# A hybrid encoder trunk on one Trainium2 core: another axis order for two copies, and a fused final norm

## The chip, the cores and the metric

The kernel runs on one core of a Trainium2 chip. The metric is the device time of one execution in microseconds (us). Before the change three executions took 2153.46, 2158.15 and 2160.55 us; the median is 2158.15 us. Engines are named as in the profile: PE is TensorE's matrix multiply and PEld its weight load, DVE is VectorE, ACT is ScalarE, POOL is GpSimd, SP is SyncE.

## The reference

For 256 tokens of width 2048 (all float32) the reference computes one layer and a final norm:

```
h = x + W_out[ norm(conv(.)) || norm(S5(.)) ](rmsnorm(x))
h = h + MemCrossAttn(rmsnorm(h), rmsnorm(mem))
h = h + PEER(rmsnorm(h))
out = rmsnorm(h)            # h * rsqrt(mean(h*h) + eps) * final_norm_g
```

The change touches PEER and the final norm. PEER has a table of 16384 experts, each with an input row u and an output row v of 2048 numbers. For each token, 8 heads choose 16 experts each, so a token has 128 chosen experts:

```
u = take(u_tab, it)                       # 128 rows of 2048 a token
act = gelu(einsum("td,tkd->tk", xt, u))
v = take(v_tab, it)
out = einsum("tk,tkd->td", gt * act, v)
```

## The kernel before

**The tokens** are handled as two tiles of 128, numbered 0 and 1 (`tt` in the code). Expert number e is written as block b = e // 128 and row r = e % 128.

**Two ways to the same scores.** Of the 2048 columns of u, the last 1280 are gathered row by row: `dot` (L857 to L862) issues an indirect DMA on POOL's queue and one multiply-and-sum on DVE, 256 times, 128 for each tile. The first 768 columns are not gathered. `dense` (L882 on) instead reads all 128 blocks of the table, transposes them on PE, and multiplies them with all tokens. This gives a score for every pair of an expert and a token, and they are kept in SBUF as `W[tt]`, 128 partitions (the row r) by 128 blocks by 128 tokens, the token innermost: `WA` for tile 0, `WB` for tile 1. Each pair of blocks ends with two ACT copies from PSUM, one for each tile (L901).

**Picking the wanted scores.** `extract` (L904) takes four tokens of a tile (a group; there are 32 groups for each tile). It loads the tokens' expert numbers with a DMA on SP's queue into one of five buffers (`id_at`), makes a selection matrix `E` on ACT (L908, L909), and multiplies it on PE with the scores of one token at a time: `W[tt][:, :, token]`, 128 by 128, is the stationary operand (L912). In that slice the 128 blocks of one token lie 128 numbers (512 bytes) apart. The result `y` goes to one of three PSUM buffers. `pick` (L916) then selects on DVE (`hit`, L920) and sums on PE (L922).

**Writing the coefficients back.** When a tile's scores are picked and the gathered part is added, `finish` gives the coefficients. `build` (L925) spreads them over a matrix of all experts, again four tokens at a time: two comparisons on DVE (L929), four scalings by a coefficient, on ACT (L936) or on DVE (L938), four products on PE (L939), and one ACT copy from PSUM into `W[tt]` (L940). The product has the token outermost and the block innermost. The copy walks in that order, so it reads PSUM in sequence and writes SBUF at steps of 512 bytes. `W[tt]` thus holds scores first and coefficients later, in the same memory.

**Order.** `settle` mixes these steps: first extract and pick for tile 0; then, for tile 1, extract, pick and `build` of tile 0's coefficients in turn. These steps are interleaved with the gathered dots: after every dot `Pace` lets 2.4 steps go, starting at dot 185 of 256 (`SETTLE_AT`, `SETTLE_RATE`). DVE's order is fixed by this program order (`manual_schedule`); the order on the other engines is chosen by the scheduler when the program is built. After the last dot, tile 1's coefficients are built in a loop by themselves (L1012 on). There, scalings alternate between ACT and DVE (`R_BY[1] = 'AVAV'`); in tile 0's builds all four are ACT's.

**The output side.** A last long loop over the 128 blocks reads the v table and multiplies it with the coefficients, `W[tt][:, b, :]`, split into high and low parts (L1062, L1063), with 18 products a block (L1072 to L1074). 576 of v's columns are gathered into `accg`, the other 1472 (three column pieces of 512, 512 and 448) are summed in PSUM.

**The final norm** (L1079 on) follows for each tile: add the PSUM sums to the residual (L1082, DVE), squares with a row sum (L1083, L1084, ACT), multiply by the gain `gF` (L1085, L1087; DVE, the last piece POOL), sum, square root and reciprocal (L1088, L110, L111), multiply by the row's scale (L1092 on ACT or L1094 on DVE), and four output DMAs on SP's queue (L1095).

Of the kernel before, what the change touches and what calls it, by code (L numbers as in the profile page):

```python
# [9 lines left out]
F32 = mybir.dt.float32  # L10
# [4 lines left out]
AF = mybir.ActivationFunctionType  # L15
ALU = mybir.AluOpType
# [4 lines left out]
P = 128  # L21
T = 256
NTT = T // P
# [29 lines left out]
DC = D - GC  # L53
COLS = [slice(c, min(c + 512, DC)) for c in range(0, DC, 512)]
NCH = len(COLS)
# [16 lines left out]
def trunk(ctx, tc, a, out, dbg=None):  # L72
    nc = tc.nc
    V, S, G, PE, SY = nc.vector, nc.scalar, nc.gpsimd, nc.tensor, nc.sync

    def bc(ap, shape):
        return ap.to_broadcast(shape)

    consts = ctx.enter_context(tc.tile_pool(name="consts", bufs=1))
    small = ctx.enter_context(tc.tile_pool(name="small", bufs=4))  # L80
# [28 lines left out]
    def rstd_of(dst, ssq, n):  # L109
        S.activation(dst, ssq, AF.Sqrt, bias=eps_t[: dst.shape[0]], scale=1.0 / n)  # L110
        V.reciprocal(dst, dst)  # L111
# [9 lines left out]
    with ExitStack() as wctx:  # L121
# [74 lines left out]
        with ExitStack() as mctx:  # L196
# [165 lines left out]
            for i, nm in enumerate(("ssm_c_re", "ssm_c_im")):  # L362
# [3 lines left out]
                for w in range(2):  # L366
                    V.tensor_scalar(cbd[:, :, w, :], craw, par[:, w:w + 1], -1.0 if i else 1.0, op0=ALU.mult,
                                    op1=ALU.mult)
# [192 lines left out]
            for k in range(CW):  # L561
                for q in range(CQ):
                    src = cpad[:, q, k:k + T]
                    if k == 0:
                        V.tensor_scalar(acc[:, q, :], src, cwT[:, q, 0:1], colv[:, 0, q:q + 1], op0=ALU.mult,
                                        op1=ALU.add)
                    else:
                        V.scalar_tensor_tensor(acc[:, q, :], src, cwT[:, q, k:k + 1], acc[:, q, :],  # L568
                                               op0=ALU.mult, op1=ALU.add)
# [4 lines left out]
            for q in range(CQ):  # L574
                S.activation(acc[:, q, :], acc[:, q, :], AF.Silu, bias=colv[:, 2, q:q + 1],
                             scale=colv[:, 1, q:q + 1])
# [287 lines left out]
    NQ = P // 4  # L864
# [11 lines left out]
    W = [wa_p.tile([P, NB, P], F32, name="WA"), WB]  # L876
# [5 lines left out]
    def dense():  # L882
        for b in range(NB):
            if b == free_blocks - free_blocks % 2:
                while (1, len(GROUPS[1]) - 1) not in ready:
                    yield
            raw = lr_p.tile([P, DU], F32, name="raw", bufs=4)
            SY.dma_start(raw, a["peer_u"][b * P:(b + 1) * P, :DU])
            pt = psu.tile([P, KD, P], F32, name="ut")
            for k in range(KD):  # L890
                PE.transpose(pt[:, k, :], raw[:, k * P:(k + 1) * P], ident)  # L891
            ut = lr_p.tile([P, KD, P], F32, name="ut", bufs=2)
            S.copy(ut, pt)  # L893
            if b % 2 == 0:
                ps = psu.tile([P, 2, T], F32, name="sy")
            for k in range(KD):
                PE.matmul(ps[:, b % 2, :], ut[:, k, :], hnT[:, k, :], start=k == 0 and b % 2 == 0,  # L897
                          stop=k == KD - 1 and b % 2 == 1, skip_group_check=True)
            if b % 2:
                for tt in range(NTT):  # L900
                    S.copy(W[tt][:, b - 1:b + 1, :], ps[:, :, tt * P:(tt + 1) * P])  # L901
            yield

    def extract(route, g):  # L904
        ids = id_at[(route.tt * NQ + g) % len(id_at)]
        SY.dma_start(ids.rearrange("p i s k -> p i (s k)"), ib_dram[route.tt][g:g + 1].to_broadcast([P, 4, 2 * NSLOT]))
        E = lr_p.tile([P, 4, P], F32, name="E", tag="ut", bufs=2)
        S.activation(E, ids[:, :, 1, :], AF.Abs, bias=part[:, 1:2], scale=1.0)  # L908
        S.activation(E, E, AF.Relu, bias=1.0, scale=-1.0)  # L909
        y = psu.tile([P, 4, P], F32, name="y", tag=("sy", "sy", "pw")[g % 3], bufs=(2, 2, 1)[g % 3])  # L910
        for i in range(4):
            PE.matmul(y[:, i, :], W[route.tt][:, :, i * NQ + g], E[:, i, :], start=i == 0, stop=i == 3,  # L912
                      skip_group_check=True)
        return ids, y

# [9 lines left out]
    def build(route, g, by, tag, bufs):  # L925
        ts = slice(4 * g, 4 * g + 4)
        LR = [lr_p.tile([P, 4, P], F32, name=nm, tag="raw", bufs=4) for nm in "RL"]
        for x, at in zip(LR, (0, 1)):
            V.tensor_tensor(x, bc(iota[:, None, :P], [P, 4, P]), bc(route.tr[:, at, ts, None], [P, 4, P]),  # L929
                            op=ALU.is_equal)  # L930
        R, L = LR
        pw = psu.tile([P, 4, P], F32, name="pw", tag=tag, bufs=bufs)
        for i in range(4):
            c = route.cT[:, 4 * g + i:4 * g + i + 1]
            if by[i] == "A":
                S.activation(R[:, i, :], R[:, i, :], AF.Copy, scale=c)  # L936
            else:
                V.tensor_scalar(R[:, i, :], R[:, i, :], c, None, op0=ALU.mult)  # L938
            PE.matmul(pw[:, i, :], L[:, i, :], R[:, i, :], start=i == 0, stop=i == 3, skip_group_check=True)  # L939
        S.copy(W[route.tt][:, :, ts].rearrange("p b t -> p t b"), pw)  # L940

    routes = [Route(0), None]
    ready = set()
# [26 lines left out]
    def settle():  # L970
        groups = P // 4
        for tt in range(NTT):
            held = {}
            for n in range(groups + LAG):
                if n < groups:
                    held[n] = extract(routes[tt], n)
                    yield
                if n >= LAG:
                    pick(routes[tt], n - LAG, *held[n - LAG])
                    yield  # L980
                if tt and n < groups:
                    build(routes[0], n, R_BY[0], "ut", 2)
                    yield
            if tt == 0:
                while tick[0] <= NSLOT:
                    yield
                yield from routes[0].finish()
# [5 lines left out]
    order = ctx.enter_context(ExitStack())  # L993
    order.enter_context(tc.manual_schedule(engines={mybir.EngineType.DVE}))
    dense_gen = dense()
    paces = [Pace(routing, ROUTE_RATE), Pace(dense_gen, DENSE_RATE)]
    tick = [0]
# [18 lines left out]
    for g in range(P // 4):  # L1016
        build(routes[1], g, R_BY[1], ("sy", "ut")[g % 2], 2)
# [10 lines left out]
    accg = [vs.tile([P, GC], F32, name=f"accg{tt}", bufs=1) for tt in range(NTT)]  # L1028
# [13 lines left out]
    def used(tt, i):  # L1042
        b = 8 + i * (D // P)
        return W[tt][:, b:b + D // P, :].rearrange("p b t -> p (b t)")

    h3, sq = ([used(tt, i) for tt in range(NTT)] for i in range(2))
    gF = used(0, 2)
# [28 lines left out]
            next(gathering)  # L1076
            done += 1

    for tt in range(NTT):  # L1079
        st = small.tile([P, NCH + 3], F32, name="rms_st")  # L1080
        for c, cs_ in enumerate(COLS):
            V.tensor_add(h3[tt][:, cs_], h3[tt][:, cs_], acc[tt][:, c, :cs_.stop - cs_.start])  # L1082
            S.activation(sq[tt][:, cs_], h3[tt][:, cs_], AF.Square, accum_out=st[:, c:c + 1])  # L1083
        S.activation(sq[tt][:, DC:], accg[tt], AF.Square, accum_out=st[:, NCH:NCH + 1])  # L1084
        V.tensor_mul(h3[tt][:, DC:], accg[tt], gF[:, DC:])  # L1085
        for c, cs_ in enumerate(COLS):
            (G if c == NCH - 1 else V).tensor_mul(h3[tt][:, cs_], h3[tt][:, cs_], gF[:, cs_])  # L1087
        V.tensor_reduce(st[:, NCH + 1:NCH + 2], st[:, :NCH + 1], axis=AX.X, op=ALU.add)  # L1088
        rstd_of(st[:, NCH + 2:NCH + 3], st[:, NCH + 1:NCH + 2], D)
        for c, cs_ in enumerate([slice(DC, D)] + COLS):  # L1090
            if c % 2:
                S.activation(sq[tt][:, cs_], h3[tt][:, cs_], AF.Copy, scale=st[:, NCH + 2:NCH + 3])  # L1092
            else:
                V.tensor_scalar(sq[tt][:, cs_], h3[tt][:, cs_], st[:, NCH + 2:NCH + 3], None, op0=ALU.mult)  # L1094
            SY.dma_start(out[tt * P:(tt + 1) * P, cs_], sq[tt][:, cs_])  # L1095


# [27 lines left out]
```

## Time and profile before

| what | us |
|---|---|
| three executions | 2158.15, 2160.55, 2153.46 |
| the profiled execution, device time | 2160.26 |
| its span, first to last instruction | 2158.2 |
| PE busy | 1985.0 (92%) |
| DVE busy | 1778.4 (82%) |
| ACT busy | 1028.6 (48%) |
| POOL busy | 751.2 (35%) |

The change touches these stretches of the span. The dense products run from about 885 to 1327 us. Tile 0's groups are extracted and picked from 1327 to 1427 us. Tile 1's groups, together with tile 0's builds, take until about 1566 us. Tile 1's builds take until 1621 us. The output loop follows until 2142 us, and the final norm ends the span. Busy shares are averages over all of it, so a stage's own rows count.

### The profile page before, as it was taken

How to read it: one execution, taken by the hardware profiler on the slowest of the kernel's cores; microseconds unless marked ns; L12 is line 12 of the kernel's file. 1: busy time of each engine (PE TensorE's matmuls, PEld its weight loads, DVE VectorE, ACT ScalarE, POOL GpSimd, SP SyncE). 2: the span in 40 equal slices, each digit the busy share in tenths (PEclk: the TensorE clock that was granted, in tenths of full speed). 3: DMA queues.
4: the chain of work that ended last, by engine and by line, in shares of the span. 5: the costliest groups of instructions: out<-in, count | busy, mean ns of one | idle time of the engine just before them, and what ended most of it. 6: DMA issues, size and time to landing. Idle time of an engine off the chain costs nothing.

```text
span 2158.2 us, 31798 instructions
## 1 busy us (share of the span) xinstructions
PE 1985.0 (92%) x11459; PEld 1714.8 (79%) x11459; DVE 1778.4 (82%) x2905; ACT 1028.6 (48%) x1683; POOL 751.2 (35%) x548
## 2 busy tenths in 40 slices
PE   8998898999999999799999997888868999999997
PEld 7987786677799888788878886777656888888886
DVE  5789999977666557999976667788897999899997
ACT  5764454446445445233333322468794444444444
POOL 0000000000000003444456666332207877677773
PEclk9999899999999999899999998798999999999998
DMA  7654444554965568799999999987618999999995
GB/s 243 169 178 147 137 144 134 167 162 146 307 204 172 170 190 283 271 306 348 325 351 401 403 400 376 336 295 260 204 68 278 361 354 335 349 335 339 338 341 197
DMA packets 199133, 567.60 MB, mean 263 GB/s; under 512 B 31537, under 2 KB 36513, under 8 KB 198848
## 3 DMA queue, kind: packets, MB, share of 16 engines
q1 hardware_dynamic: 141632, 322.27, 45.5%
q0 software_dynamic: 57344, 243.30, 30.0%
q8 instruction: 90, 1.47, 0.3%
q14 instruction: 67, 0.55, 0.1%
HBM read 553.57 MB, written 11.93 MB: 262 GB/s over the span
## 4 chain that ended last, share of the span: by engine, by line
PE 45%; DVE 25%; issue 13%; DMA 8%; POOL 6%; ACT 3%; SPq 0%; POOLq 0%; ACTq 0%; DVEq 0%
PE acc L1073 7%; PE acc L1074 7%; PE acc L1072 7%; POOL u L859 5%; DVE u L861 5%; DVE acc L568 3%; DVE w_lo L163 3%; PE mm L183 3%; PE mm L181 3%; PE mm L182 3%; PE y L912 3%; PE mm L173 2%; PE mm L174 2%; PE mm L172 2%; DMA hnT<-ib_dram 1%
## 5 line engine op out<-in xcount | busy, mean ns | idle before, releaser
L861 DVE SCALAR_TENSOR_TENSOR u<-u,hnF 128x1280 f32<-128x1280 f32 x256 | 388.4, 1519 | 85.7 <-DMA u<-in_peer_u,uidx 84.3
L1037 POOL DMA_INDIRECT v<-in_peer_v,vidx x256 | 387.3, 1513 | 192.0 <-ACT WB L940 72.4
L859 POOL DMA_INDIRECT u<-in_peer_u,uidx x256 | 318.3, 1243 | 342.4 <-DVE u L861 259.6
L162 ACT CAST w_hi<-w_raw 128x1024 fp32r<-128x1024 f32 (+2 forms) x228 | 231.4, 1018 | 289.3 <-PE mm L182 128.6
L897 PE MATMUL sy<-hnT,ut 128*128 128x256 f32 x1536 | 353.4, 382 | 8.7 <-ACT ut L893 7.2
L163 DVE TENSOR_TENSOR w_lo<-w_raw,w_hi 128x1024 fp32r<-128x1024 f32 (+2 forms) x228 | 268.6, 1181 | 107.4 <-ACT w_hi L162 107.2
L897 PEld LDWEIGHTS sy<-hnT,ut 128*128 128x128 f32 x1536 | 284.9, 191 | 48.6 <-ACT ut L893 11.4
L103 ACT CAST vh<-vr 128x1472 fp32r<-128x1472 f32 x128 | 183.1, 1430 | 265.3 <-PE acc L1073 206.7
L1073 PE MATMUL acc<-vh,wl 128*128 128x512 f32 (+1 forms) x768 | 296.6, 386 | 5.0 <-DVE wl L1063 4.6
L183 PE MATMUL mm<-aT_hi,w_lo 128*128 128x256 f32 x960 | 272.3, 292 | 27.6 <-DVE w_lo L163 27.3
L1074 PE MATMUL acc<-vl,wh 128*128 128x512 f32 (+1 forms) x768 | 295.1, 386 | 0.0
L742 POOL TENSOR_TENSOR hnT<-aT_hi,aT_lo 128x1024 f32<-128x1024 f32 (+1 forms) x2 | 4.1, 2080 | 817.9 <-ACT w_hi L162 817.9
L181 PE MATMUL mm<-aT_hi,w_hi 128*128 128x256 f32 x960 | 277.0, 291 | 3.7 <-DVE sg L264 2.3
L1072 PE MATMUL acc<-vh,wh 128*128 128x512 f32 (+1 forms) x768 | 276.7, 385 | 3.5 <-ACT vh L103 2.5
L182 PE MATMUL mm<-aT_lo,w_hi 128*128 128x256 f32 x960 | 274.5, 288 | 0.0
L104 DVE TENSOR_TENSOR vl<-vr,vh 128x1472 fp32r<-128x1472 f32 x128 | 216.5, 1692 | 40.4 <-ACT vh L103 38.5
L1039 DVE SCALAR_TENSOR_TENSOR accg<-v,coef,accg 128x576 f32<-128x576 f32 x256 | 208.6, 815 | 11.0 <-DMA v<-in_peer_v,vidx 5.5
L183 PEld LDWEIGHTS mm<-aT_hi,w_lo 128*128 128x128 f32 x960 | 184.1, 196 | 35.9 <-DVE w_lo L163 32.9
L181 PEld LDWEIGHTS mm<-aT_hi,w_hi 128*128 128x128 f32 x960 | 186.6, 195 | 7.7 <-DVE sg L264 2.9
L182 PEld LDWEIGHTS mm<-aT_lo,w_hi 128*128 128x128 f32 x960 | 187.0, 195 | 1.3 <-issue 0.4
L893 ACT COPY ut<-ut 128x768 f32<-128x768 f32 x128 | 100.3, 801 | 168.7 <-PE ut L891 145.9
L1073 PEld LDWEIGHTS acc<-vh,wl 128*128 128x128 f32 x768 | 145.2, 189 | 36.3 <-DVE wl L1063 5.3
(335 smaller groups left out, 3426.2 us busy)
## 6 DMA issues: line engine op xcount, KB each, us to landing
vr<-in_peer_v SPq DMA_DIRECT2D x128, 736.0 KB
raw<-in_peer_u SPq DMA_DIRECT2D x128, 384.0 KB
w_raw<-in_w_kv_mem SPq DMA_DIRECT2D x64, 512.0 KB
w_raw<-in_w_in SPq DMA_DIRECT2D x48, 512.0 KB
w_raw<-in_w_out SPq DMA_DIRECT2D x32, 512.0 KB
w_raw<-in_w_q_mem SPq DMA_DIRECT2D x32, 512.0 KB
w_raw<-in_w_o_mem SPq DMA_DIRECT2D x32, 512.0 KB
hnT<-ib_dram SPq DMA_DIRECT2D x38, 256.0 KB
```

The lines of the kernel that those rows point to most:

```text
L162: S.copy(hi, raw)
L163: V.tensor_sub(lo, raw, hi.bitcast(F32))
L181: PE.matmul(o, wh, ah, start=first and cb % 2 == 0, stop=False, skip_group_check=True)
L182: PE.matmul(o, wh, al, start=False, stop=False, skip_group_check=True)
L183: PE.matmul(o, wl, ah, start=False, stop=last and end, skip_group_check=True)
L859: G.indirect_dma_start(out=u, out_offset=None, in_=a["peer_u"].rearrange("e (q c) -> (e q) c", c=GU), in_offset=bass.IndirectOffsetOnAxis( ...
L861: V.scalar_tensor_tensor(u, u, 1.0, hnF[:, self.tt, :], op0=ALU.mult, op1=ALU.mult, accum_out=self.act[:, j:j + 1])
L897: PE.matmul(ps[:, b % 2, :], ut[:, k, :], hnT[:, k, :], start=k == 0 and b % 2 == 0, stop=k == KD - 1 and b % 2 == 1, skip_group_check=True)
L1037: G.indirect_dma_start(out=v, out_offset=None, in_=table, in_offset=bass.IndirectOffsetOnAxis(ap=vidx[tt][:, j:j + 1], axis=0))
L1072: PE.matmul(o, wh[:, tt, :], vh[:, cs_], start=b == 0, stop=False)
L1073: PE.matmul(o, wl[:, tt, :], vh[:, cs_], start=False, stop=False)
L1074: PE.matmul(o, wh[:, tt, :], vl[:, cs_], start=False, stop=b == NB - 1)
```

## The change

The scores of tile 0 are stored with the token outermost and the block innermost; those of tile 1 stay as they were. The coefficients of both tiles stay block by block, but the copy that writes them walks over blocks, with the four tokens innermost. In the final norm, gain and row scale are applied in one DVE instruction for three of the four column pieces; the last piece has the gain on DVE and the scale on ACT. Both tiles' sums come first, then both tiles' outputs. POOL has no part in the final norm any more.

```diff
             if b % 2:
-                for tt in range(NTT):
-                    S.copy(W[tt][:, b - 1:b + 1, :], ps[:, :, tt * P:(tt + 1) * P])
+                S.copy(W[0][:, :, b - 1:b + 1], ps[:, :, :P].rearrange("p b t -> p t b"))
+                S.copy(W[1][:, b - 1:b + 1, :], ps[:, :, P:])
...
-            PE.matmul(y[:, i, :], W[route.tt][:, :, i * NQ + g], E[:, i, :], start=i == 0, stop=i == 3,
+            PE.matmul(y[:, i, :], W[1][:, :, i * NQ + g] if route.tt else W[0][:, i * NQ + g, :], E[:, i, :], start=i == 0, stop=i == 3,
...
-        S.copy(W[route.tt][:, :, ts].rearrange("p b t -> p t b"), pw)
+        S.copy(W[route.tt][:, :, ts], pw.rearrange("p t b -> p b t"))
...
-    for tt in range(NTT):
-        st = small.tile([P, NCH + 3], F32, name="rms_st")
+    sts = [small.tile([P, NCH + 3], F32, name="rms_st") for _ in range(NTT)]
+    for tt, st in enumerate(sts):
         for c, cs_ in enumerate(COLS):
             V.tensor_add(h3[tt][:, cs_], h3[tt][:, cs_], acc[tt][:, c, :cs_.stop - cs_.start])
             S.activation(sq[tt][:, cs_], h3[tt][:, cs_], AF.Square, accum_out=st[:, c:c + 1])
         S.activation(sq[tt][:, DC:], accg[tt], AF.Square, accum_out=st[:, NCH:NCH + 1])
-        V.tensor_mul(h3[tt][:, DC:], accg[tt], gF[:, DC:])
-        for c, cs_ in enumerate(COLS):
-            (G if c == NCH - 1 else V).tensor_mul(h3[tt][:, cs_], h3[tt][:, cs_], gF[:, cs_])
         V.tensor_reduce(st[:, NCH + 1:NCH + 2], st[:, :NCH + 1], axis=AX.X, op=ALU.add)
         rstd_of(st[:, NCH + 2:NCH + 3], st[:, NCH + 1:NCH + 2], D)
+    for tt, st in enumerate(sts):
         for c, cs_ in enumerate([slice(DC, D)] + COLS):
-            if c % 2:
-                S.activation(sq[tt][:, cs_], h3[tt][:, cs_], AF.Copy, scale=st[:, NCH + 2:NCH + 3])
+            src = h3[tt][:, cs_] if c else accg[tt]
+            if c == NCH:
+                V.tensor_mul(sq[tt][:, cs_], src, gF[:, cs_])
+                S.activation(sq[tt][:, cs_], sq[tt][:, cs_], AF.Copy, scale=st[:, NCH + 2:NCH + 3])
             else:
-                V.tensor_scalar(sq[tt][:, cs_], h3[tt][:, cs_], st[:, NCH + 2:NCH + 3], None, op0=ALU.mult)
+                V.scalar_tensor_tensor(sq[tt][:, cs_], src, st[:, NCH + 2:NCH + 3], gF[:, cs_], op0=ALU.mult,
+                                       op1=ALU.mult)
             SY.dma_start(out[tt * P:(tt + 1) * P, cs_], sq[tt][:, cs_])
```

## Rows read from the trace of the kernel before

**Rows 1.** The page's chain that ended last, shares of the span by engine.

```profile
PE 45%; DVE 25%; issue 13%; DMA 8%; POOL 6%; ACT 3%; SPq 0%; POOLq 0%; ACTq 0%; DVEq 0%
```

**Rows 2.** Stretches: length, each engine's busy us (instructions), PE clock, DMA share, GB/s.

```profile
core 0: us, PE busy (x) PEld busy (x) DVE busy (x) ACT busy (x) POOL busy (x), PEclk, DMA share, GB/s
...
1200.00:1326.00 126.00, 120.73 (x646) 104.90 (x645) 85.27 (x113) 39.49 (x73) 81.02 (x56) 1.00 1.01 397
...
1345.40:1425.50 80.10, 70.16 (x480) 57.82 (x480) 58.45 (x85) 38.41 (x57) 29.11 (x27) 0.80 0.95 330
1425.50:1566.60 141.10, 118.56 (x777) 101.67 (x777) 126.22 (x191) 107.57 (x225) 41.00 (x39) 0.89 0.71 240
...
1700.00:2142.00 442.00, 442.00 (x1997) 374.88 (x1996) 401.04 (x553) 201.50 (x332) 326.25 (x213) 1.00 0.92 333
```

**Rows 3.** Waits, 1346 to 1427 and 1427 to 1566 us: total, times, longest.

```profile
DVE hit L920 <- PE y L912: 20.6, 15, 2.8
...
DVE L L929 <- PE pw L939: 11.1, 12, 1.9
...
PE pw L939 <- ACT R L936: 17.7, 22, 1.8
```

**Rows 4.** Groups of PE by line, in stretches 1327:1425, 885:1330 and 1565:1640.

```profile
L912 PE MATMUL y<-E,WA 128*128 128x128 f32 x256 | 63.6, 411 | 5.6 <-ACT E L909 5.2 <-ACT WA L901 0.5
...
L922 PE MATMUL more<-hit,onecol 128*32 128x128 f32 x248 | 15.3, 326 | 17.0 <-DVE hit L920 17.0
...
L891 PE MATMUL ut<-ident,raw 128*128 128x128 f32 x762 | 101.9, 275 | 3.2 <-DMA raw<-in_peer_u 3.2
...
L939 PE MATMUL pw<-R,L 128*128 128x128 f32 x256 | 37.5, 293 | 14.4 <-ACT R L936 13.9 <-DVE L L929 0.6
```

**Rows 5.** Low clock: all engines, PE in time, and tile pw alone (PE, PEld, ACT).

```profile
1380.00:1384.00 4.00, 4.00 (x23) 3.62 (x24) 2.62 (x4) 1.81 (x3) 0.94 (x1) 0.50 0.91 262
...
1380.58 3.64 PE L912 MATMUL y<-E,WA 128*128 128x128 f32 x15
...
1564.00:1572.00 8.00, 3.04 (x14) 3.05 (x15) 0.93 (x1) 0.50 0.43 127
```

**Rows 6.** Chain of waits in order of time: an index load on the path.

```profile
1358.60 6.25 DMA hnF<-ib_dram
```

**Rows 7.** ACT's copies out of PSUM by line and form: busy us, mean ns, idle before.

```profile
L940 ACT COPY WB<-pw 128x512 f32<-128x512 f32 x32 | 33.4, 1043 | 1.7 <-PE pw L939 1.7
...
L901 ACT COPY WA<-sy 128x256 f32<-128x256 f32 x64 | 23.9, 373 | 120.4 <-PE sy L897 112.4 <-DVE WB L791 5.3 <-issue 2.6
...
L491 ACT COPY kv_ev<-mm 128x512 f32<-128x512 f32 x8 | 4.7, 587 | 20.5 <-PE mm L143 20.3 <-DMA k_dram<-kv_ev 0.2
```

**Rows 8.** Tile 1's builds: one stretch, and two copies in order of time.

```profile
1580.00:1585.00 5.00, 3.59 (x26) 2.91 (x25) 5.00 (x13) 5.00 (x10) 0.00 (x0) 1.00 0.00 0
...
1577.36 1.03 ACT L940 COPY WB<-pw 128x512 f32<-128x512 f32 x1
...
1578.96 1.04 ACT L940 COPY WB<-pw 128x512 f32<-128x512 f32 x1
```

**Rows 9.** The final norm in order of time, and one group of the last 50 us.

```profile
2142.23 1.82 DVE L1082 TENSOR_TENSOR WA<-WA,acc 128x512 f32<-128x512 f32 x3 [2.18 <-PE acc L1074]
...
2147.27 2.21 DVE L1087 TENSOR_TENSOR WB<-WB,WA 128x512 f32<-128x512 f32 x2
2147.31 1.28 ACT L110 ACT_TABLE_LOAD   x1
...
2150.20 1.81 SPq L1095 DMA_DIRECT2D out<-WA  x4
...
2151.56 0.65 ACT L1092 ACTIVATE WB<-WB,rms_st 128x448 f32<-128x448 f32 x1
...
2152.10 2.64 SPq L1095 DMA_DIRECT2D out<-WB  x4
...
L1039 DVE SCALAR_TENSOR_TENSOR accg<-v,coef,accg 128x576 f32<-128x576 f32 x14 | 11.4, 816 | 0.2
```

## The prediction, made before the changed kernel ran

> **What bounds the kernel now.** I read the chain of waits on the page first. It is mostly PE, then DVE, with ACT at 3% [rows 1]. The change acts on a few stages only, so I then asked for busy time by stretch [rows 2], and for what each engine waited on in those stretches [rows 3].
>
> In the output loop PE is busy 442.00 of 442 us. The change does not touch that loop, but whatever an earlier stage gains or loses moves its start, and so reaches the end in full.
>
> From 1345.4 to 1425.5 us tile 0's 32 groups are picked. DVE is busy for 58.45 of 80.10 us. It waits 20.6 us for PE's y, that is for L912, and for almost nothing else [rows 3]. So here PE's 256 L912 instructions set the pace (80.1 / 32 = 2.50 us a group).
>
> From 1425.5 to 1566.6 us tile 1's groups are picked and tile 0's coefficients built. DVE is busy 126.22 of 141.10 us, and 11.1 us of its 14.9 idle us are waits for the build's PE product, which itself waited 17.7 us for ACT's scalings. DVE is the bound, with ACT (107.57 us busy) a little behind.
>
> The last two places, tile 1's builds and the final norm, I read instruction by instruction below.
>
> **Part 1: tile 0's scores token by token.** L912 is two instructions a product, eight a group. They take 63.6 / 256 = 0.248 us each [rows 4], 1.99 us a group. Two other PE lines have the same shape, 128 by 128 float32, but a stationary operand that lies in sequence: L891 takes 101.9 / 762 = 0.134 us and L939 37.5 / 256 = 0.146 us. So the slice with steps of 512 bytes costs about 0.1 us an instruction, and the change removes those steps for tile 0. At 0.14 a group falls to 1.1 us. Those prices are for the full clock. At the low level (granted clock 0.50, 1.2 GHz) a strided one takes 3.64 / 15 = 0.243 us, no more than at full clock, and one in sequence 3.04 / 14 = 0.217 [rows 5]; there a group falls only to 1.74 us. I take the full clock, because tile 1's builds run at 1.00 with PE busy only 3.59 of 5 us [rows 8], and the picking stage will stay about as busy as that.
>
> What is late next? Four limits for the 80.1 us:
> - PE: 32 x (1.1 + 15.3 / 32 for L922) = 51 us.
> - DVE: its own work, 58.45 us.
> - The five index buffers: a buffer is free after `hit`, then comes its load, 6.25 us when it showed on the path [rows 6], then two ACT steps (about 1.3 us), y (1.1) and `hit` (0.75). That is 9.4 us for five groups, 1.9 a group, 60 us.
> - DMA: the stage moves 330 GB/s x 80.1 us = 26.4 MB. The fastest stretch of the dense stage moved 397 GB/s at a share of 1.01 [rows 2]. At that rate 26.4 MB take 66.5 us.
>
> The largest gives a gain of 80.1 - 66.5 = 13.6 us. Limits so close together rarely overlap perfectly, so I take 12. The bounds are 0 (the loads slow down as they come closer together) and 21.6 (DVE saturated). POOL's gather issues are not a limit: 29.11 us busy. What follows on DVE simply moves forward; it has no due time of its own.
>
> The price is paid at L901. The copy of tile 0's scores now reads PSUM at steps of a block and writes pairs of numbers 512 bytes apart. The trace has no such copy; the nearest are the plain one, 0.373 us, and L940, whose strided writes cost (1.043 - 0.587) / 512 = 0.9 ns a number [rows 7]. By that it is 0.37 to 0.60 us; with a strided read that costs as much again, 0.83. I take 0.60, nearest to L940. 64 copies add 15 us (at most 29) to ACT, which is busy 39.49 of 126 us in that stage while PE is busy 120.73: hidden. It also ends before it matters: the dense products end at about 1327 us, and DVE's first `hit` opens the next stretch only at 1345.4 [rows 2]. Without that cover it would be 64 x 0.23 = 15 us.
>
> **Part 2: coefficient copies with four tokens inside.** 64 copies cost 1.04 us each; a plain copy of this size costs 0.587 [rows 7]. The new one writes four numbers in sequence (16 bytes) but reads PSUM at steps of 512 bytes, which no row shows. Bounds: 0.587 below; above, 0.587 plus twice the present extra, 1.5 us. I take 0.65, by the row of the plain copy: the runs of four should remove most of the write's cost.
>
> [...]
>
> In tile 1's builds the copies sit 1.60 us apart, with ACT busy 5.00 of 5 us, but DVE is busy 5.00 of 5 too [rows 8]. A shorter copy leaves DVE's 1.6 us as the period: gain 0 here. In the stage before, DVE's 11.1 us of waits for the build's product shrink, because ACT reaches its scalings up to 0.4 us earlier in each of 32 builds. ACT saves 13 us of work; I count a third, 4 us (bounds 0 and 11, if the copy gets no dearer).
>
> **Part 3: the final norm.** PE's last product for tile 0 releases DVE at 2142.23, and the last output DMA is issued by 2152.10 + 2.64 = 2154.74 [rows 9]. The last data piece is ready at 2152.21, but SP still has to send issues of 0.45 to 0.66 us each in turn, eight in all from 2150.20. So the issue of the first piece counts as much as the last piece.
>
> After the change, DVE has the six sums first (until about 2145.8, six at 0.6), and no multiplications by the gain ahead of the square root. The row scale of tile 0 needs its squares, which trail its three sums (done at 2144.05) by an estimated 1.3 us, then the table load (1.28) and a root and reciprocal (an estimated 0.5): about 2147.2, instead of after the last multiplication by the gain, 2149.48. Then each tile has one fused instruction of 576 (0.82, as L1039) and two of 512 (about 0.7), with a multiplication of 448 (0.6) put in an earlier gap. DVE is through with tile 0 at 2149.4 and with tile 1 at about 2151.5. The SP issues start near 2148 and keep up, so the last is sent at about 2152.5: 2 us earlier. If ACT runs tile 1's squares before the root, the root comes at 2148.9, tile 1 ends at 2153.3, and the gain is under 1 us. I take 2; bounds -1 and 3.
>
> **Sum.** 12 + 4 + 0 + 2 = 18 us off the profiled execution's 2160.3 us (span 2158.2 and 2.1 around it) gives 2142.3. That execution was 2.1 us above the median of the runs, so the forecast for the median is 2140.
>
> **Rivals.**
> 1. The copy is not cheaper (1.04 us): the strided read costs what the strided write did. For it: no row shows such a read. Part 2 falls to 0: gain 14, median 2144.
> 2. PE's gain is taken back in the picking stage. The DMA share is already 0.95, and at that stage's own rate a gain needs more than 330 GB/s; and if PE, with shorter work, falls to the low clock, a group costs 1.74 + 0.66 us on PE and the stage 77 us, a gain of 3. Against it: 397 GB/s was reached, and the builds keep the full clock at 72% busy. With 1 us of part 2 and 1 of part 3 the gain is about 5: median 2153.
> 3. The new copy is dearer. It decides in tile 1's builds, where ACT has no slack: each 0.1 us above 1.04 adds 3.2 us there and about half as much in the stage before. At 1.33 us the 14 us of the other parts are gone. At the upper bound, 1.5 us, the builds take 32 x 0.46 = 15 us more and the stage before 7: 2160.3 - 14 + 22 = 2168, median 2166. For it: the steps of the read are as wide as those of the write were. Against it: one side is now nearly in sequence, where before one side was entirely strided, and that price was 1.04.
>
> **How the numbers follow.** The forecast has 0.60, rival 1 0.14, rival 2 0.17, rival 3 0.09. A change under 0.3% (6.5 us) cannot be told from none here. Rival 2 straddles that bound: 0.07 faster, 0.10 same. Rival 3 gives 0.07 slower, 0.02 same. So faster 0.81, same 0.12, slower 0.07. The time is the forecast's, 2140. The range runs from 2128 (DVE saturated while picking, most of part 2's waits gone, a gain of 30) to 2154 (rival 2); outside lie rival 3, part of rival 2 and a little below.
>
> **What would show it.** Right: L912 on WA at 0.13 to 0.15 us an instruction, WB's as before; `hit`'s wait for y from 20.6 to under 8 us; the stage from 80 to about 68 us; L940 near 0.65 us with the period in tile 1's builds still 1.6 us and ACT no longer full; the output loop unchanged in length. Wrong: a granted clock near 0.5 in the picking stage, DVE waiting for u's DMA or ACT for the index loads instead of PE; L940 at 1.04 or above with a longer period; or an end-of-span that gains or loses elsewhere, as by another order of the scheduler.

## The result, and the profile after

The changed kernel takes 2144.39 us (median of 10 runs, 2138.47 to 2149.99), the kernel before 2155.82 us (median of 10 runs, 2150.73 to 2160.55). The ratio is 0.9949, 95% interval 0.9938 to 0.9961: 11 us less, between 8 and 13. The forecast was 2140.

The two profiled executions differ by more, 2139.49 against 2160.26 us, because one lies low and the other high among its runs. 4.7 us of the difference arise before the dense products start (877.2 against 881.9 us), where nothing was changed. So stages are compared below, not totals.

| stage, by its first and last event | before, us | after, us |
|---|---|---|
| dense products to DVE's first `hit` | 463.6 | 463.6 |
| tile 0's picking: first `hit` to tile 0's coefficients (L848) | 82.0 | 74.0 |
| tile 1's picking with tile 0's builds: to tile 1's coefficients | 139.8 | 134.0 |
| tile 1's builds: to the last L939 | 52.5 | 52.7 |
| output loop: first L1072 to first sum of the norm (L1082) | 519.6 | 518.1 |
| final norm: first L1082 to the end of the span | 16.0 | 15.7 |

These cuts are at DVE's instructions. The stretches in [rows 2] and in the expectations end where PE starts tile 1's first product, which PE does a little earlier or later as it runs ahead. The output loop's 1.5 us lie within its scatter: 517.8 to 519.6 us over all runs below.

The two picking stages in stretches, edges rounded to 0.1 us (same columns as [rows 2]), first the kernel before:

```profile
1345.50:1427.50 82.00, 72.09 (x495) 59.55 (x496) 59.98 (x88) 39.34 (x59) 29.32 (x28) 0.80 0.94 329
1427.50:1567.30 139.80, 116.63 (x763) 99.94 (x763) 124.96 (x188) 106.93 (x224) 40.69 (x39) 0.88 0.71 238
```

and the changed kernel:

```profile
1340.80:1414.80 74.00, 56.36 (x495) 42.59 (x496) 59.77 (x88) 39.20 (x59) 28.98 (x28) 0.82 0.97 358
1414.80:1548.70 133.90, 113.87 (x763) 98.50 (x762) 124.58 (x188) 95.06 (x224) 40.08 (x38) 0.92 0.75 250
```

DVE's work is the same as before; PE's is 16 us less in the first stage, ACT's 12 us less in the second. Beside [rows 4] and [rows 7], the groups of PE and ACT that the change touches:

```profile
L912 PE MATMUL y<-E,WB 128*128 128x128 f32 x256 | 64.3, 399 | 2.0 <-ACT E L909 1.1 <-issue 0.9
L912 PE MATMUL y<-E,WA 128*128 128x128 f32 x256 | 45.5, 335 | 12.3 <-ACT E L909 11.3 <-ACT WA L900 0.5
...
L900 ACT COPY WA<-sy 128x256 f32<-128x256 f32 x64 | 24.9, 388 | 124.4 <-PE sy L897 124.4
...
L940 ACT COPY WA<-pw 128x512 f32<-128x512 f32 x32 | 18.6, 582 | 15.8 <-PE pw L939 15.4
L940 ACT COPY WB<-pw 128x512 f32<-128x512 f32 x32 | 18.1, 565 | 2.5 <-PE pw L939 2.5
```

WB, still strided, stays at 64.3 us (64.5 before); WA falls from 63.6 to 45.5. One y of tile 0 where the granted clock was 1.00, eight instructions in order of time:

```profile
1364.81 1.16 PE L912 MATMUL y<-E,WA 128*128 128x128 f32 x8 [0.26 <-ACT E L909]
```

The waits of the first picking stage, in the form of [rows 3], first ACT's in the kernel before:

```profile
ACT E L908 <- DMA hnF<-ib_dram: 20.2, 6, 14.1
...
ACT E L908 <- DMA hnT<-ib_dram: 5.3, 4, 2.3
```

and the changed kernel:

```profile
ACT E L908 <- DMA hnF<-ib_dram: 20.9, 10, 13.0
...
ACT E L908 <- DMA hnT<-ib_dram: 13.6, 12, 1.9
DVE hit L920 <- PE y L912: 11.0, 15, 2.8
```

DVE's wait for y fell from 20.6 to 11.0 us. ACT's waits for index loads (tiles hnF and hnT) rose from 25.5 to 34.5 us. In each kernel one long wait, 14.1 and 13.0 us, begins before the stage and ends with the first load after the first `hit`; without it they rose from 11.4 to 21.5 us. Between 1359 and 1393 us the chain of waits, in order of time, goes from one index load to the next. Before that it goes mostly through the gathered rows u and DVE, after it mostly through y. Part of it:

```profile
1366.21 6.64 DMA hnF<-ib_dram
...
1372.93 0.73 ACT E L908
...
1373.69 0.64 ACT E L909
...
1374.37 1.80 PE y L912 x8
...
1376.19 0.76 DVE hit L920
...
1377.00 7.21 DMA hnF<-ib_dram
...
1384.29 0.73 ACT E L908
...
1385.60 7.36 DMA hnT<-ib_dram
```

One period of tile 1's builds, in order of time (compare [rows 8]). ACT has 0.43 us idle, DVE none:

```profile
1573.55 0.69 DVE L929 TENSOR_TENSOR R<-iota,tr 128x512 f32<-128x512 f32 x1
1574.15 0.69 DVE L929 TENSOR_TENSOR L<-iota,tr 128x512 f32<-128x512 f32 x1
1574.28 0.69 ACT L936 ACTIVATE R<-R,cT 128x128 f32<-128x128 f32 x2 [0.43 <-DVE R L929]
1574.76 0.48 DVE L938 TENSOR_SCALAR R<-R,cT 128x128 f32<-128x128 f32 x2
1574.88 0.56 ACT L940 COPY WB<-pw 128x512 f32<-128x512 f32 x1
...
1575.15 0.69 DVE L929 TENSOR_TENSOR R<-iota,tr 128x512 f32<-128x512 f32 x1
```

The final norm (compare [rows 9]). Tile 1's last square ends before ACT loads the table for the root, and DVE's first fused instruction starts 7 us after the first sum:

```profile
2121.91 1.82 DVE L1082 TENSOR_TENSOR WA<-WA,acc 128x512 f32<-128x512 f32 x3 [2.85 <-PE acc L1074]
...
2126.32 0.56 ACT L1083 ACTIVATE WB<-WB 128x448 f32<-128x448 f32 x1
...
2126.99 1.28 ACT L110 ACT_TABLE_LOAD   x1
...
2128.88 0.80 DVE L1094 SCALAR_TENSOR_TENSOR WA<-accg,rms_st,WA 128x576 f32<-128x576 f32 x1
...
2132.01 1.97 SPq L1096 DMA_DIRECT2D out<-WB  x3
```

### The profile page after: what moved, and what is told of

Its sections match the earlier page's. It is cut to its first block, busy times and chain, and to the rows that moved or that the text cites. A ratio compares the mean times of both kernels' runs of the same rounds, so it can differ in the third digit from the quotient of the medians.

```text
span 2137.6 us, 31790 instructions
## 1 busy us (share of the span) xinstructions
PE 1970.1 (92%) x11459; PEld 1699.6 (80%) x11459; DVE 1776.7 (83%) x2903; ACT 1002.5 (47%) x1681; POOL 736.9 (34%) x546
## 4 chain that ended last, share of the span: by engine, by line
PE 47%; DVE 23%; issue 12%; DMA 9%; POOL 6%; ACT 3%; SPq 0%; POOLq 0%; DVEq 0%; ACTq 0%
PE acc L1073 8%; PE acc L1074 8%; PE acc L1072 8%; POOL u L859 5%; DVE u L861 5%; PE mm L183 4%; PE mm L181 4%; PE mm L182 4%; DVE acc L568 3%; DVE w_lo L163 3%; DMA hnT<-ib_dram 2%; PE mm L173 2%; PE mm L174 2%; PE mm L172 2%; DMA hnF<-ib_dram 1%
## 5 line engine op out<-in xcount | busy, mean ns | idle before, releaser
L859 POOL DMA_INDIRECT u<-in_peer_u,uidx x256 | 311.2, 1216 | 338.7 <-DVE u L861 262.9
L163 DVE TENSOR_TENSOR w_lo<-w_raw,w_hi 128x1024 fp32r<-128x1024 f32 (+2 forms) x228 | 277.2, 1219 | 106.9 <-ACT w_hi L162 103.1
L1072 PE MATMUL acc<-vh,wh 128*128 128x512 f32 (+1 forms) x768 | 277.1, 385 | 2.7 <-ACT vh L103 2.2
```

What stands on the lines that cost most here:

```text
L163: V.tensor_sub(lo, raw, hi.bitcast(F32))
L859: G.indirect_dma_start(out=u, out_offset=None, in_=a["peer_u"].rearrange("e (q c) -> (e q) c", c=GU), in_offset=bass.IndirectOffsetOnAxis( ...
L1072: PE.matmul(o, wh[:, tt, :], vh[:, cs_], start=b == 0, stop=False)
```

## The experiments

All ratios are to the kernel before on the same chip. The stages are cut as in the table above.

| run | timed ratio (95% interval) | tile 0's picking | tile 1's picking | builds | norm |
|---|---|---|---|---|---|
| before | | 82.0 | 139.8 | 52.5 | 16.0 |
| changed | 0.9949 (0.9938 to 0.9961) | 74.0 | 134.0 | 52.7 | 15.7 |
| scores alone | 0.9959 (0.9945 to 0.9973) | 72.9 | 138.6 | 52.5 | 16.0 |
| copies alone | 0.9993 (0.9981 to 1.0005) | 82.5 | 135.6 | 52.5 | 16.0 |
| norm alone | 0.9999 (0.9985 to 1.0012) | 82.6 | 137.9 | 52.5 | 15.7 |
| changed, without copies | 0.9960 (0.9946 to 0.9974) | 74.3 | 138.1 | 52.6 | 15.7 |
| changed, three scalings on ACT | 0.9915 (0.9897 to 0.9932) | 71.1 | 135.9 | 47.0 | 15.6 |
| changed, half index bytes | 0.9942 (0.9922 to 0.9962) | 71.8 | 133.6 | 52.5 | 15.6 |
| changed, a second time | 0.9944 (0.9925 to 0.9963) | 74.6 | 133.5 | 52.5 | 15.7 |
| changed, eight index buffers | 0.9936 (0.9921 to 0.9951) | 66.5 | 135.0 | 52.4 | 15.6 |
| the three improvements together | 0.9888 (0.9868 to 0.9908) | 67.9 | 135.8 | 47.0 | 13.6 |

### Part 1 alone

```diff
-                for tt in range(NTT):
-                    S.copy(W[tt][:, b - 1:b + 1, :], ps[:, :, tt * P:(tt + 1) * P])
+                S.copy(W[0][:, :, b - 1:b + 1], ps[:, :, :P].rearrange("p b t -> p t b"))
+                S.copy(W[1][:, b - 1:b + 1, :], ps[:, :, P:])
...
-            PE.matmul(y[:, i, :], W[route.tt][:, :, i * NQ + g], E[:, i, :], ...
+            PE.matmul(y[:, i, :], W[1][:, :, i * NQ + g] if route.tt else W[0][:, i * NQ + g, :], E[:, i, :], ...
```

> The kernel before with part 1 alone (tile 0's scores token by token, L900 and L912); coefficient copies and final norm as before. Theory: part 1 is the larger half of the gain. L912 on WA falls from 0.248 to about 0.15 us an instruction at full clock, and the stretch from DVE's first hit to tile 1's first product from 80 to about 72 us, where the index loads and DMA take over as the limit; the stage after it keeps its 141 us. Total 8 us less, ratio about 0.996. Rival: the picking stage gains, but the stage after it loses as much, since its index loads and gathers bunch up; total within 2 us of before, ratio 0.999 to 1.001.

2147.06 us, ratio 0.9959: 9 us less by the ratio. The first picking stage takes 72.9 us against 82.0, the next one 138.6 against 139.8. The theory holds and the rival falls: nothing is given back in the next stage.

### Part 2 alone

```diff
-        S.copy(W[route.tt][:, :, ts].rearrange("p b t -> p t b"), pw)
+        S.copy(W[route.tt][:, :, ts], pw.rearrange("p t b -> p b t"))
```

> The kernel before with part 2 alone (coefficient copies with four tokens innermost). Theory: L940 falls from 1.04 to about 0.57 us; tile 1's builds keep their 1.6 us period because DVE is full; the stage in which tile 0's builds are mixed with tile 1's picking gains 4 to 6 us, through DVE's waits for the build's product (11.1 us before). Total 4 to 6 us less, ratio 0.997 to 0.998. Rival: what that stage gained in the changed kernel came from part 1 (its index loads start earlier), and the copies give nothing: total within 2 us of before, ratio 0.999 to 1.001.

The groups of ACT for the copies in this run:

```profile
L940 ACT COPY WA<-pw 128x512 f32<-128x512 f32 x32 | 18.6, 581 | 16.3 <-PE pw L939 16.0
L940 ACT COPY WB<-pw 128x512 f32<-128x512 f32 x32 | 18.1, 565 | 2.2 <-PE pw L939 2.2
```

The copy's price and the unchanged builds (52.5 us) came as expected, and the stage took 135.6 us against 139.8. That stage scatters, though: in the run with the norm alone nothing of it is changed, and it takes 137.9 us. The timed gain, 1.5 us with an interval from 4 less to 1 more, is below the theory's 4 to 6 and does not settle it by itself.

### The changed kernel without part 2

The diff is the one above, reversed, on the changed kernel.

> The changed kernel with the old coefficient copy (token outermost, 1.04 us), parts 1 and 3 kept. A second measurement of what part 2 is worth, beside the copies-only run (timed 0.9993 of before, with an interval that allows 0 to 4 us; 3.7 us in the stage of tile 0's builds by the traces). Theory: that stage takes 135 to 137 us instead of 131 to 133, tile 1's builds stay at 57, total 4 us above the changed kernel, ratio to before about 0.9965. Rival: the stage's length is within its own scatter and part 2 is worth nothing: 131 to 133 us and 0.995.

2147.10 us, ratio 0.9960, against 0.9949 and 0.9944 for the changed kernel: 2 to 3 us more, less than the 4 expected and within the scatter of the intervals. The traces speak more clearly. The four runs with the old copy have 139.8, 137.9, 138.6 and 138.1 us in that stage (mean 138.6). The four with the new copy and five index buffers whose index loads are whole have 135.6, 134.0, 135.9 and 133.5 (mean 134.8), with no overlap: 3.8 us. In that stage DVE's wait for the build's product is 11.5 us here:

```profile
DVE L L929 <- PE pw L939: 11.5, 12, 2.3
```

and in the changed kernel

```profile
DVE L L929 <- PE pw L939: 6.3, 9, 1.7
```

### Part 3 alone

The diff is the final norm's part of the change, on the kernel before.

> The kernel before with part 3 alone (the final norm fused). Theory: ACT still runs all six squares before the table load and the root, so from DVE's first add to the end of the span it takes 15.7 us against 16.0, and the total stays within 1 us, ratio 0.9995 to 1.0005. Rival, the forecast: 2 us less, ratio 0.999.

2155.28 us, ratio 0.9999: no change that can be measured. The norm takes 15.7 us against 16.0, as the theory had it.

### Three scalings on ACT in tile 1's builds

```diff
-R_BY = ('AAAA', 'AVAV')
+R_BY = ('AAAA', 'AAAV')
```

> The changed kernel with one more scaling on ACT in tile 1's builds (R_BY[1] 'AAAV' for 'AVAV'). Theory: those builds are bound by DVE at 1.6 us (two comparisons at 0.6, two scalings at 0.2), and ACT now has 0.43 us idle a build; with three scalings on ACT, DVE needs 1.4 and ACT 0.9 + 0.55 = 1.45 us. Period 1.45 us, 32 x 0.15 = 5 us less than the changed kernel, ratio to before about 0.9925. Rival: the period is set by the buffers between the engines or by the product's wait for the scalings, not by DVE's sum: it stays at 1.6 us and the ratio at 0.995.

2136.97 us, ratio 0.9915. The builds take 47.0 us against 52.5. One period in order of time:

```profile
1572.39 0.68 DVE L929 TENSOR_TENSOR R<-iota,tr 128x512 f32<-128x512 f32 x1
...
1572.59 0.56 ACT L940 COPY WB<-pw 128x512 f32<-128x512 f32 x1
1572.99 0.68 DVE L929 TENSOR_TENSOR L<-iota,tr 128x512 f32<-128x512 f32 x1
1573.10 0.99 ACT L936 ACTIVATE R<-R,cT 128x128 f32<-128x128 f32 x3
1573.59 0.27 DVE L938 TENSOR_SCALAR R<-R,cT 128x128 f32<-128x128 f32 x1
...
1573.79 0.68 DVE L929 TENSOR_TENSOR R<-iota,tr 128x512 f32<-128x512 f32 x1
```

1.40 us from one R to the next, where it was 1.60: DVE's sum set the period. That the third scaling fits on ACT only with the cheaper copy is argued, not run: with the old copy ACT was already busy 5.00 of 5 us [rows 8]. The shown part of the gain is the builds' 5.5 us; the median moved by more, with six runs.

### What limits tile 0's picking now

First, half the bytes in each index load:

```diff
-        SY.dma_start(ids.rearrange(...), ib_dram[route.tt][g:g + 1].to_broadcast([P, 4, 2 * NSLOT]))
+        n = 4 if route.tt == 0 and g < 5 else 2
+        SY.dma_start(ids[:, :n].rearrange(...), ib_dram[route.tt][g:g + 1, :n].to_broadcast([P, n, 2 * NSLOT]))
```

> The changed kernel, but from the sixth group on each index load brings the numbers of only two of its four tokens (128 KB for 256 KB), the other two being left from an earlier group; so the picked scores of those tokens are wrong. Question: what limits tile 0's picking stage now (72.4 us in the changed kernel, DVE's own work 58.4, DMA share 0.97). Theory A, DMA rate: bytes fall from 26.1 to about 22 MB, and the stage falls to DVE's bound, 60 to 63 us. Theory B, the loop of five index buffers (load 6 to 7 us, two ACT steps, product, pick): the load gets a little shorter, stage 67 to 70 us. Either way 3 to 12 us less than the changed kernel, ratio to before 0.989 to 0.993.

The stage takes 67.3 us by the cut of the expectation, which is Theory B's range, and 71.8 by DVE's cut. The five traces with whole loads, five buffers and the new scores have 69.8 to 73.0 and 71.1 to 74.6 by these cuts, so only the first cut shows a gain. The ratio is 0.9942, no different from the changed kernel's. A DMA rate as the limit is not borne out: by neither cut did the stage fall to Theory A's 60 to 63 us, and it moved only 331 GB/s.

Then more index buffers at the same bytes:

```diff
+    for i in range(3):
+        x = lr_p.tile([P, 512], F32, name=f"ids{i}", bufs=1)
+        id_at.append(x.bitcast(BF16).rearrange("p (i s k) -> p i s k", i=4, s=2))
```

> The changed kernel with eight index buffers instead of five (three more tiles of 512 float32); same bytes, same instructions. Theory A, DMA rate: the stage stays at 69 to 72 us, with DMA share 0.97 or above, and the total at the changed kernel's, ratio to before about 0.995. Theory B, the loop of five buffers: loads start three groups earlier, ACT's waits for index loads (34 us in the changed kernel) mostly go, the stage falls to 60 to 63 us, and the total by about 9 us, ratio about 0.991.

By mistake the kernel that ran under this expectation was the changed kernel itself, without that diff. It is a second measurement of it: 2143.80 us, ratio 0.9944, 74.6 and 133.5 us in the two stages. The run with the diff followed:

> The changed kernel with eight index buffers instead of five, and nothing else (the run e6_eight_index_buffers was by mistake the changed kernel itself). Theory B, the loop of five buffers: the picking stage falls from 71 to 73 us to 62 to 65, as in e9_best; DVE's waits for y from 11 to about 5.5 us; total about 8 us less than the changed kernel if the stage after it keeps its 131 to 133 us, ratio to before about 0.991. Rival C: the loads that come earlier crowd the next stage, which then takes 135 to 136 us as in e9_best, so only 4 to 5 us are left, ratio about 0.993. Theory A, DMA rate (70 us or more) is held for unlikely since e9_best.

The stage takes 62.0 us by the cut of the expectation and 66.5 by DVE's, against 74.0 and 74.6: 8 us less. Its stretch and ACT's and DVE's waits in it:

```profile
1345.50:1411.90 66.40, 54.30 (x504) 41.41 (x504) 59.19 (x87) 40.73 (x62) 29.82 (x28) 0.89 1.02 399
```

```profile
ACT E L912 <- DMA hnT<-ib_dram: 4.8, 5, 1.5
...
DVE hit L924 <- PE y L916: 4.0, 5, 2.0
ACT E L912 <- DMA ids<-ib_dram: 2.5, 3, 1.6
ACT E L912 <- DMA hnF<-ib_dram: 2.5, 2, 1.6
```

(L912, L916 and L924 are here what L908, L912 and L920 are elsewhere.) ACT's waits for index loads are 9.8 us, where the changed kernel had 21.5 without the one long wait (that one is put down to y here). So the loop of five buffers was the limit of this stage in the changed kernel. With eight, the stage moves 399 GB/s at a share of 1.02, as much as the last stretch of the dense stage in [rows 2], and a load takes 10.8 us from its issue until ACT uses it, where it took 7.2. So now the DMA rate may be what is left; DVE is busy 59 of 66 us. The next stage takes 135.0 us, within the 133.5 to 135.9 of the others with the new copy, so Rival C is neither shown nor excluded.

The timed ratio, 0.9936, is only 2 to 3 us better than the changed kernel's. A longer cut has less than 8 us too: from the first dense product to tile 1's coefficients this run takes 667.7 us and the last run below 668.6, against 670.7 to 672.7 in the three traces with all three parts of the change, five buffers and whole loads. In this run DVE's first `hit` comes later, 466.2 us after the first dense product against 463.6; over all runs that time scatters from 461.8 to 468.3. So the stage's 8 us are shown, but not that all of them reach the end.

### Together, with the norm's order written out

The changed kernel with both diffs above, and in the final norm ACT kept to the order of the program (tile 0's squares, its root, then tile 1's):

```diff
+    last = ctx.enter_context(ExitStack())
+    last.enter_context(tc.manual_schedule(engines={mybir.EngineType.Activation}))
     sts = [small.tile([P, NCH + 3], F32, name="rms_st") for _ in range(NTT)]
     for tt, st in enumerate(sts):
+        S.activation(sq[tt][:, DC:], accg[tt], AF.Square, accum_out=st[:, NCH:NCH + 1])
         for c, cs_ in enumerate(COLS):
...
-        S.activation(sq[tt][:, DC:], accg[tt], AF.Square, accum_out=st[:, NCH:NCH + 1])
...
+    last.close()
```

> The changed kernel with three scalings on ACT in tile 1's builds, eight index buffers, and in the final norm ACT's order written out: tile 0's squares, its root, then tile 1's squares. Builds 51.5 us as in the run with three scalings on ACT. Picking stage as in the run with eight buffers alone. Final norm: tile 0's row scale comes about 1.5 us earlier than in the changed kernel, and DVE's fused instructions start at once on tile 0; from DVE's first add to the end 14 us against 15.7 (if the forecast's order argument holds; a rival is that tile 1's squares, now behind the table load, make tile 1's output late by as much: 15.5 to 16). Total ratio to before 0.987 to 0.991, against 0.9915 for three scalings alone.

2131.66 us, ratio 0.9888: 24 us less than before, the fastest of all. The norm takes 13.6 us. Its rows:

```profile
2117.47 1.82 DVE L1089 TENSOR_TENSOR WA<-WA,acc 128x512 f32<-128x512 f32 x3 [2.85 <-PE acc L1078]
...
2119.90 0.19 ACT L1090 ACTIVATION_READ_ACCUMULATOR WA<-WA 128x1 f32 x1
2120.11 1.28 ACT L110 ACT_TABLE_LOAD   x1
...
2121.93 0.82 DVE L1100 SCALAR_TENSOR_TENSOR WA<-accg,rms_st,WA 128x576 f32<-128x576 f32 x1
...
2125.81 1.80 SPq L1102 DMA_DIRECT2D out<-WB  x4
```

ACT loads the table right after tile 0's squares. DVE starts its first fused instruction 4.5 us after its first sum, where the changed kernel took 7.0, and SP sends the last output 2 us earlier relative to the first sum.

## Why the prediction was right or wrong

**Part 1, 12 us.** Direction and mechanism right, size 9: the six traces with the scores token by token and five index buffers (one of them with half the bytes) have 71.1 to 74.6 us, the three with the old scores 82.0 to 82.6. Two of the signs of being right fell short: `hit`'s wait for y is 11.0 us (under 8 forecast), and the stage by the forecast's own cut 72.4 us (about 68). One sign of being wrong came, ACT waiting for the index loads.

The step that failed is the list of four limits, in which the loop of five index buffers had 9.4 us for five groups, 1.9 a group. In the trace of the changed kernel one lap, from the `hit` that frees a buffer to the next `hit` on it, takes 11.4 us (mean over groups 9 to 32), 2.3 a group. Its terms: 7.2 us from the issue of a load until ACT uses it (4.6 to 9.8), priced at 6.25 by one load; 1.5 for the two ACT steps (1.3); 1.3 for y (1.1); 0.75 for `hit`; and 0.7 of waits between these steps, which the sum put at nothing. The trace before the change had the same mean of 7.2 us for these loads. A lap of five buffers takes five times as long as a group whatever the limit is, so its length proves nothing by itself. But only 0.7 us of it are waits for an engine (1.6 before the change), and the run with eight buffers shows that the index loop, not the DMA rate, was the largest of the four.

The price of an instruction in sequence held at full clock (1.16 us for the eight of one y), but over the stage it was 45.5 / 256 = 0.178 us, at a granted clock of 0.82. The forecast took 1.00 from tile 1's builds, while the row of this stage itself had 0.80 before the change [rows 2]. In y this is 0.2 us of the lap; what the low clock costs beyond that was not tried.

**The price at L901** was taken as 0.60 us and is 0.388. It was hidden, as said, as far as the traces can tell: ACT idles 124.4 us before these copies, waiting for PE. From the first dense product to DVE's first `hit` both kernels take 463.6 us, but that they agree so closely is chance: the eight traces with the new copy of the scores scatter from 461.8 to 468.3 us (mean 464.7), the three with the old one have 463.6 to 464.1.

**Part 2, 4 us.** Price 0.565 to 0.582 us (0.65 taken), builds unchanged with DVE as their bound, and 3.8 us in the stage before: right by the traces, though the timings alone show 1.5 to 3 with intervals that reach zero. The third of ACT's saving that the forecast counted was a guess between 0 and 11 us, so that the size fits is partly luck. Rivals 1 and 3, a strided read as dear as the strided write or dearer, are refuted: the new copy costs what the plain one of the same size did, 0.587 [rows 7]. The Trainium skill (SBUF — State Buffer, Door 1: The DMA port swizzle) says that accesses which stay in one 16-byte line of SBUF, four float32, run at full bandwidth. This trace agrees: the copy that writes four in sequence took 0.565 to 0.582 us, the one that writes single numbers 1.04.

**Part 3, 2 us.** Wrong in size: 0.3. The step that failed is the order on ACT. The forecast had the root of tile 0 before tile 1's squares and named the other order as worth under 1 us; the other order is what the scheduler chose. With the order written out, the norm takes 13.6 us, 2.4 less than before and 2.1 less than in the changed kernel.

**The sum.** By the traces 9 + 4 + 0 + 0.3 = 13, by the timings 11 (8 to 13), against 18. The single-part runs add up to 9 + 1.5 + 0 = 10.5 us, so the timings show no interaction of the parts. Rival 2 was partly there: at a granted clock of 0.82 and with the index loads on the path some 3 of part 1's 12 us did not come, but not the whole gain was lost. The forecast of the time, 2140, is off by 4.4 us and that of the gain by 7: the three runs before, from which it started, had a median 2.3 us above that of the ten, and this hid part of the miss.

## What to carry to other kernels

When one wait is taken out of a loop of buffers, price the whole lap (load, each engine's step, the waits between them, release) with the mean of many loads of that stage, not with one of them. Where two engines are both full, work saved on one of them shows no gain at first, but it leaves room to move work over from the other: the cheaper copy gave nothing in the builds until one scaling moved from DVE to ACT, and then the builds were 5.5 us shorter. Where a gain hangs on the order of two instructions on one engine, look at the order that was built, or write it out.

## What the runs showed of the hardware that was not expected

An ACT copy that writes single float32 numbers 512 bytes apart takes 1.04 us for 512 numbers a partition [rows 7]. One that writes four in sequence and reads PSUM at steps of 512 bytes takes 0.57 to 0.58, and the plain one 0.587. Pairs already do nearly as well: the copy of 256 numbers in pairs 512 bytes apart takes 0.388 us against 0.373 in sequence.

A PE instruction whose stationary operand, 128 by 128 float32, lies at steps of 512 bytes takes about 0.25 us at either level of the clock (0.248 as a mean over the stage, 0.243 at a granted clock of 0.50). In sequence it takes 0.145 at the full level (1.16 / 8) and 0.217 to 0.225 at the low one (3.04 / 14 and 1.80 / 8).
